# Where the attention block's output stage meets the second MLP: sixteen transposes put ahead of fifteen filling products, and shift and scale given out by whole PSUM tiles

## The chip, the cores and the metric

The kernel runs on one core of a Trainium2 chip. A core has five engines with a queue each: TensorE (PE in the profile), VectorE (DVE), ScalarE (ACT), GpSimd (POOL) and SyncE (SP), the last of which issues nearly all transfers here. Every time is in microseconds (us) of the device; less is better. Before the change three runs took 1163.52, 1165.8 and 1166.83 us; their median is 1165.8 us.

## The reference, cut to what matters

Two layers act on 512 latent tokens and 256 context tokens of width 1024. Layer 0 mixes tokens by pooling, layer 1 by attention; an MLP follows each. The stretch around the change belongs to layer 1 and the latent tokens alone:

```
o_lat = attend(q_l, k_all, v_all).reshape(B, L, D) @ w_o
x     = x + gt1 * rms_norm(o_lat, g_mix_post)
h     = rms_norm(x, g_mlp_pre) * (1.0 + sc2) + sh2      # modulate
m_lat = square(relu(h @ w_mlp_in)) @ w_mlp_out
```

The norm goes over a token's 1024 values, the shift and the scale are per channel. So a row of 128 tokens must have all of its attention output before it can be normalised, and the MLP's first product needs it transposed, with channels on the partitions.

## The kernel before

The 512 latent tokens are four tiles of 128, t = 0 to 3. Float32 operands are split into a coarse part ("hi") and a remainder ("lo"), and each product of 128 channels is three matmuls: hi by hi, hi by lo, lo by hi. ScalarE makes hi by a cast, VectorE makes lo by a subtraction.

`output()` is the output stage. `attn_mm` multiplies the attention result with w_o (line 1403, tile `psy`), `attn_ev` applies the gate and sums squares. Then, tile by tile, `norm_r` adds the residual (VectorE, line 364), `norm_s` sums squares (ScalarE, line 196) and has GpSimd make the reciprocal root (`rs`, line 211), and `norm_c` scales the row into `acc` (ScalarE line 560 or VectorE line 562). For t = 3, the last, `norm_c` is on VectorE.

When two tiles stand ready, `norm_pair` calls `modulated_pair`. It makes 16 transposes of 128x128 (TensorE, line 385) into four PSUM tiles `psx`. Each tile q holds channels 2q and 2q+1 (kk = 0 and 1), each over both token tiles (u = 0 and 1). Eight operations of 128x256 then apply scale and shift and write back to `acc` (VectorE line 393, ScalarE line 396; the tuple `on_act` says which goes where). The two results of tile q overwrite half a row of `acc` (512 columns): q = 0 and 1 the halves of the pair's first token tile, q = 2 and 3 those of its second. So an operation must also wait until the transposes that read those columns are through: q = 1 overwrites what channels 4 to 7 of the first token tile are transposed from. For the last pair (`fine`) each q then gets its own cast to hi (ScalarE, line 399) and subtraction to lo (VectorE, line 400).

The second MLP takes its inner products from `Inner.part` (line 608, tile `psin`), 128x256 each here: chunk 0 is the tokens of pair 0 and 1, chunk 1 those of pair 2 and 3. Since pair (0, 1) is ready earlier, chunk 0 serves as filling while the last pair is normalised: 24 matmuls for each of the two halves of the first weight tile (`first1[0]`) and 24 for the first half of the second (`first1[1]`), 72 in all. All that follows them needs the last pair: 120 more matmuls of 128x256, then `mlp1` with matmuls of 128x512. There, fourteen of the sixteen weight tiles are worked in seven pairs, each with seven products (`product`, lines 987 to 991; tile `pso`), whose sums ScalarE stores for the first pair (line 989) and VectorE adds for the others (line 991).

The order of the work comes from two things. The program is written with a table of times (`at(time, fn)`, run in the order of time), and the framework then schedules the instructions of each engine by its own estimate of their times. Where a list `ordered` holds True, `Kept` marks each TensorE instruction so that it stays in the order of the program; such instructions carry line 87 in the profile. In `output()` it held False. `norm_pair` of the last pair stood at 47.4, and the filling of `first1[1]` behind it at 47.5 and 47.6.

Of the kernel before, what the change touches and what calls it, by code (L numbers as in the profile page):

```python
# [19 lines left out]
KT = D // P  # L20
# [44 lines left out]
class Steps:  # L65
# [3 lines left out]
    def at(self, t, fn, *args):  # L69
        self.items.append((t, len(self.items), fn, args))  # L70
# [20 lines left out]
def backbone(ctx: ExitStack, tc, x, ctx_in, w_ada, w_pool, pool_scale, w_qkv, g_q, g_k, w_o, w_mlp_in,  # L91
             w_mlp_out, vecs, rope, band, out):
    nc = tc.nc
    ordered, mixed = [False], [False]
# [48 lines left out]
    def raw_load(src, pool=None):  # L143
        if pool is None and turns:
            pool = (pools[0], rawp)[turns.pop(0)]
        t = (pool or pools[0]).tile([P, 2048], F32, tag="raw", name="raw")
        d = sy.dma_start(t, src)
        if pinned[0]:
            tc.keep_in_program_order(d)
        return t  # L150
# [12 lines left out]
    def split(raw, hi, lo, pin=False, q=None):  # L163
        if q is not None:
            raw, hi, lo = (z[:, 512 * q:512 * q + 512] for z in (raw, hi, lo))
        a = sc.copy(hi, raw)  # L166
        if pin:
            tc.keep_in_program_order(a)
        b = ve.tensor_tensor(out=lo, in0=raw, in1=hi, op=ALU.subtract)  # L169
        if pin:  # L170
            tc.keep_in_program_order(b)
# [248 lines left out]
    def mod0(t, q, on_act):  # L420
        ci, ps = 0 if t < NL else 1, turned[t, q]
        for kk in range(2):
            k = 2 * q + kk
            sa, b = avec[0][1][:, k, ci:ci + 1], mods[0][:, SH2 * KT + k, ci:ci + 1]
            h, src = accv[:, t:t + 2, k * P:(k + 1) * P], ps[:, kk, :].rearrange("p (u n) -> p u n", n=P)
            if on_act:
                sc.activation(h, src, AF.Identity, scale=sa, bias=b)
            else:
                ve.tensor_scalar(out=h, in0=src, scalar1=sa, scalar2=b, op0=ALU.mult, op1=ALU.add)
        ks = slice(2 * q, 2 * q + 2)  # L430
        h = accv[:, t:t + 2, 2 * q * P:(2 * q + 2) * P].rearrange("p u (k n) -> p k u n", n=P)
        turned[t, q] = (h, *(z.rearrange("p k (h q n) -> p k q h n", h=2, n=P)[:, ks, t // 2] for z in (hH, hL)))
# [329 lines left out]
    def w_in(i, g, rg, pin=False, wait=None):  # L762
        return rg.load(w_mlp_in[i, g], 256, pin, wait)
# [49 lines left out]
    def halved(t, q, part):  # L813
        h, hi, lo = turned[t, q]
        if part:
            ve.tensor_tensor(out=lo, in0=h, in1=hi, op=ALU.subtract)
        else:
            sc.copy(hi, h)

    def keep(store, key, fn, *args):  # L820
# [16 lines left out]
        h=lambda t, act, q: mod0(t, q, act), xhi=lambda t, q: halved(t, q, 0), xlo=lambda t, q: halved(t, q, 1))  # L837
# [391 lines left out]
    def last0(st, n, t):  # L1229
# [18 lines left out]
        if n == 5:  # L1248
            st.at(18.4, rope_load)
            st.at(44, rope_tables)  # L1250
            st.at(5.5, lambda: split(*raw0[0], True))
            raws = []
            st.at(31.3, w_chunk, 2, 1, raws)
            for q in range(4):
                st.at(31.3 + q / 1000, lambda q: split(*raws[0], q=q), q)
            st.at(52, w_chunk, 0, 0, raws)
            st.at(52.01, lambda: split(*raws[1], True))
            st.at(61, w_chunk, 0, 1, raws)
            st.at(61.01, lambda: split(*raws[2], True))
            st.at(61.1, w_chunk, 1, 0, raws)  # L1260
            st.at(61.11, lambda: split(*raws[3], True))
            st.at(83, w_chunk, 1, 1, raws)
            st.at(83.01, lambda: split(*raws[4], True))
            attention(st, 97.4, 2.7)
            output(st, 97.4 + 2.7 * 43.691)
# [150 lines left out]
    first1, raw1 = [], []  # L1416
# [38 lines left out]
    def output(st, base):  # L1455
        at, halves = lambda i, fn, *args: st.at(base + i, fn, *args), []
        for n, (ch, t) in enumerate(((0, 0), (0, 1), (1, 0), (0, 2), (1, 1), (0, 3), (1, 2), (1, 3))):
            b = 5.2 * n
            at(b, attn_mm, ch, t)
            at([5.2, 10.4, 15.6, 20.8, 26, 31.2, 36.4, 41.6][n], attn_ev, ch, t)  # L1460
            if ch:
                at([16.9, 27.3, 37.7, 42.9][t], norm_r, t, (False, False, False, False)[t])
                at([17.9, 28.3, 38.7, 43.9][t], norm_s, t, (False, False, False, False)[t])
                at([18.814, 29.214, 39.614, 46.4][t], norm_c, t, (False, True, True, False)[t])
                if t % 2:
                    at(36.3 if t == 1 else 47.4, norm_pair, t - 1, 1, 1, h1H, h1L, t == 1, t == 3,
                       ((False, True, True, False, True, False, True, False), (True, False, True, False, True, False, True, False))[t // 2], halves if t == 1 else None)

        def upper_half():
            hi, lo, h = halves[0]  # L1470
            tc.keep_in_program_order(sc.copy(hi, h))
            ve.tensor_tensor(out=lo, in0=h, in1=hi, op=ALU.subtract)

        at(41.65, upper_half)
        for f in range(2):
            for h in range(2):
                at(41.7 + f / 10 + h, lambda *a: first1[0].part(*a), 0, f, range(4 * h, 4 * h + 4))
        parts[1] = small.tile([P, 32], F32, tag="part", name="part", bufs=1)
        for j in range(4):
            at((7, 12, 17, 25)[j], ada_sum, 1, GT2, j, 1, parts[1][:, 8 * j:8 * j + 8])  # L1480
        raws = []
        at(20, lambda: first1.append(Inner(0, w_in(1, 0, early, False, raws), h1H, h1L, None, chunks1, LAT, True)))
        at(32, lambda: split(*raws[0]))
        at(26, lambda: raw1.append(raw_load(w_mlp_in[1, 1], rawp).rearrange("p (k n) -> p k n", n=256)))
        at(36, half_early)
        for h in range(2):
            at((47.5, 47.6)[h], lambda ks: first1[1].part(0, 0, ks), range(4 * h, 4 * h + 4))

    def fin_b(t):
        y = yg.pop(t)  # L1490
# [94 lines left out]
```

## Time and profile before

| what | us |
|---|---|
| median of three runs | 1165.8 |
| the profiled execution, as timed | 1165.75 |
| its span, first to last instruction | 1163.9 |
| around the span | 1.85 |
| TensorE busy | 1143.8 (98%) |
| VectorE busy | 933.6 (80%) |
| ScalarE busy | 628.5 (54%) |
| granted TensorE clock, mean | 0.996 |

Busy times are sums over the span. A matmul is listed with its whole passage through the array, while the next one starts before its end; so the distance between two starts is what a matmul costs in a row of them. In a row of the timeline the first number is the start, the second the time from the first start to the last end of the group, and brackets give the engine's idle time ahead of the group with what ended it.

### The profile page before, as it was taken

How to read it: one execution, taken by the hardware profiler on the slowest of the kernel's cores; microseconds unless marked ns; L12 is line 12 of the kernel's file. 1: busy time of each engine (PE TensorE's matmuls, PEld its weight loads, DVE VectorE, ACT ScalarE, POOL GpSimd, SP SyncE). 2: the span in 40 equal slices, each digit the busy share in tenths (PEclk: the TensorE clock that was granted, in tenths of full speed). 3: DMA queues.
4: the chain of work that ended last, by engine and by line, in shares of the span. 5: the costliest groups of instructions: out<-in, count | busy, mean ns of one | idle time of the engine just before them, and what ended most of it. 6: DMA issues, size and time to landing. Idle time of an engine off the chain costs nothing.

```text
span 1163.9 us, 15946 instructions
## 1 busy us (share of the span) xinstructions
PE 1143.8 (98%) x6172; PEld 993.2 (85%) x6172; DVE 933.6 (80%) x1515; ACT 628.5 (54%) x1068; POOL 70.0 (6%) x120
## 2 busy tenths in 40 slices
PE   7999999999999999999999999999999999999997
PEld 5679889998898988998888889988988888888886
DVE  4688688998988997996778699867688779778876
ACT  5687555554354534555675367743676436534522
POOL 2130000000000000000241200002000000000001
PEclk9999999999999999999999999999999999999999
DMA  9964223343334444343522002125234214313312
GB/s 372 419 251 168 73 85 105 142 145 122 132 145 145 145 145 145 109 145 109 181 73 73 37 1 73 37 77 210 76 133 157 75 70 145 109 41 140 109 39 106
DMA packets 25516, 147.32 MB, mean 127 GB/s; under 512 B 2785, under 2 KB 5217, under 8 KB 9698
## 3 DMA queue, kind: packets, MB, share of 16 engines
q1 hardware_dynamic: 25442, 146.32, 34.5%
q8 instruction: 48, 0.79, 0.3%
q14 instruction: 26, 0.21, 0.1%
HBM read 138.96 MB, written 7.34 MB: 126 GB/s over the span
## 4 chain that ended last, share of the span: by engine, by line
PE 62%; issue 30%; DVE 2%; POOL 2%; ACT 2%; DMA 1%; POOLq 0%; SPq 0%; DVEq 0%; ACTq 0%
PE pso L878 22%; PE psin L732 18%; PE psy L1403 3%; PE po L1378 3%; PE pss L1337 3%; PE psq L1133 2%; PE pspt L1359 2%; PE pspool L87 2%; PE psin L87 1%; PE psin L608 1%; PE psada L87 1%; DMA raw<-in_w_ada 1%; PE psm L87 1%; PE psg L87 1%; POOL rs L211 1%
## 5 line engine op out<-in xcount | busy, mean ns | idle before, releaser
L878 PE MATMUL pso<-units,rb 128*128 128x512 f32 x1152 | 278.9, 392 | 0.0
L878 PEld LDWEIGHTS pso<-units,rb 128*128 128x128 f32 x1152 | 214.7, 188 | 41.1
L301 DVE SCALAR_TENSOR_TENSOR rows<-raw,cond,rows 128x256 f32<-128x256 f32 x280 | 127.3, 479 | 2.0
L890 DVE TENSOR_TENSOR acc<-acc,pso 128x512 f32<-128x512 f32 x129 | 85.5, 677 | 41.9 <-PE pso L878 41.6
L608 PE MATMUL psin<-ra,rb 128*128 128x512 f32 (+1 forms) x320 | 91.4, 363 | 1.4 <-ACT ra L399 1.4
L987 PE MATMUL pso<-units,pairs 128*128 128x512 f32 x336 | 82.3, 389 | 0.0
L608 PE MATMUL psin<-ra 128*128 128x512 f32 (+1 forms) x256 | 76.2, 376 | 0.0
L987 PEld LDWEIGHTS pso<-units,pairs 128*128 128x128 f32 x336 | 63.1, 188 | 13.1
L991 DVE TENSOR_TENSOR acc<-acc,pso 128x512 f32<-128x512 f32 x72 | 48.8, 684 | 26.5 <-PE pso L987 26.5
L608 PEld LDWEIGHTS psin<-ra,rb 128*128 128x128 f32 x320 | 58.4, 193 | 10.3 <-ACT ra L399 1.6
L209 POOL TENSOR_SCALAR ms<-ss 128x1 f32<-128x1 f32 x16 | 10.5, 655 | 939.1 <-ACT junk L196 925.4
L732 PE MATMUL psin<-ra,units 128*128 128x384 f32 x336 | 65.5, 337 | 0.4 <-ACT psin L744 0.4
L732 PE MATMUL psin<-sums,units 128*128 128x384 f32 x336 | 64.0, 337 | 0.0
L732 PEld LDWEIGHTS psin<-ra,units 128*128 128x128 f32 x336 | 59.8, 188 | 3.9 <-ACT psin L744 0.5
L169 DVE TENSOR_TENSOR units<-raw,units 128x1024 fp32r<-128x1024 f32 (+2 forms) x49 | 55.1, 1152 | 8.6 <-ACT units L166 8.4
L732 PEld LDWEIGHTS psin<-sums,units 128*128 128x128 f32 x336 | 59.0, 188 | 1.6
L608 PE MATMUL psin<-rb 128*128 128x512 f32 (+1 forms) x160 | 58.0, 363 | 0.2 <-DVE rb L400 0.2
L166 ACT CAST units<-raw 128x1024 fp32r<-128x1024 f32 (+2 forms) x49 | 46.9, 996 | 17.9 <-PE pso L878 13.7
L608 PEld LDWEIGHTS psin<-ra 128*128 128x128 f32 x256 | 47.1, 188 | 8.7
L888 ACT COPY acc<-pso 128x512 f32<-128x512 f32 x48 | 27.1, 586 | 48.2 <-PE pso L878 47.7
L1133 PE MATMUL psq<-units,ra 128*128 128x512 f32 x216 | 52.2, 393 | 0.0
L608 PE MATMUL psin<-rb,ra 128*128 128x512 f32 (+1 forms) x128 | 48.1, 376 | 0.0
(282 smaller groups left out, 2384.8 us busy)
## 6 DMA issues: line engine op xcount, KB each, us to landing
raw<-in_w_ada SPq DMA_DIRECT2D x48, 1024.0 KB, 5.0
raw<-in_w_mlp_in SPq DMA_DIRECT2D x32, 1024.0 KB, 4.8
raw<-in_w_mlp_out SPq DMA_DIRECT2D x32, 1024.0 KB, 5.7
raw<-in_w_qkv SPq DMA_DIRECT2D x6, 1024.0 KB, 4.8
spill<-xr SPq DMA_DIRECT2D x10, 512.0 KB, 4.1
xr<-spill SPq DMA_DIRECT2D x10, 512.0 KB, 6.7
raw<-in_w_o SPq DMA_DIRECT2D x4, 1024.0 KB, 4.9
xr<-in_x SPq DMA_DIRECT2D x4, 512.0 KB, 5.7
```

Of the source, the lines that this page charges most:

```text
L87: return lambda *args, **kw: self.tc.keep_in_program_order(f(*args, **kw))
L166: a = sc.copy(hi, raw)
L169: b = ve.tensor_tensor(out=lo, in0=raw, in1=hi, op=ALU.subtract)
L301: ve.scalar_tensor_tensor(out=r, in0=raw[:, k, :], scalar=cond[:, k, c:c + 1], in1=r, op0=ALU.mult, op1=ALU.add)
L608: te.matmul(ps[:, bank, o:o + ln], w[:, k, fs], rhs, start=start, stop=(k == KT - 1 and n == 2), skip_group_check=len(ks) < KT or self.paired)
L732: te.matmul(bank, w[k], a[k], start=start and k == 0 and m == 0, stop=stop and k == 3 and m == 2, skip_group_check=True)
L878: te.matmul(pss[h][:, 0:cols[h][1]], a[:, f, ts_], w[:, f, cols[h][0]:sum(cols[h])], start=(n == 0 and not seeded[t]), stop=(n == len(seq) ...
L890: ve.tensor_tensor(out=d, in0=d, in1=ps[:, 0:w], op=ALU.add)
L987: te.matmul(ps, a, w, start=(m == 0), stop=(m == len(seq) - 1))
L991: ve.tensor_tensor(out=M[n][:, t], in0=M[n][:, t], in1=ps, op=ALU.add)
L1133: te.matmul(ps, a[:, k, sl], w[:, k % 4, :], start=(k == 0 and n == 0), stop=(k == KT - 1 and n == 2))
L1337: te.matmul(ps[:, c2, 0:384], a[:, sl], b[:, kv, 384 * c2:384 * c2 + 384], start=(n == 0), stop=(n == 2))
```

## The change

Three things change in `output()`. The shift and scale of the last pair is given out by whole PSUM tiles: q = 0 and 2 to ScalarE, q = 1 and 3 to VectorE, four operations each as before. The filling products of `first1[1]` are cut into 9 (channels 0 to 2), now at 47.3 ahead of the pair's transposes, and 15 (channels 3 to 7), at 47.45 behind them. From 47.35 to 47.5 `ordered` holds True, so that the 16 transposes and the 15 products stay in this order among themselves.

```diff
@@ -1464,7 +1464,7 @@
                 if t % 2:
                     at(36.3 if t == 1 else 47.4, norm_pair, t - 1, 1, 1, h1H, h1L, t == 1, t == 3,
-                       ((False, True, True, False, True, False, True, False), (True, False, True, False, True, False, True, False))[t // 2], halves if t == 1 else None)
+                       ((False, True, True, False, True, False, True, False), (True, True, False, False, True, True, False, False))[t // 2], halves if t == 1 else None)
@@ -1484,7 +1484,9 @@
         for h in range(2):
-            at((47.5, 47.6)[h], lambda ks: first1[1].part(0, 0, ks), range(4 * h, 4 * h + 4))
+            at((47.3, 47.45)[h], lambda ks: first1[1].part(0, 0, ks), (range(3), range(3, KT))[h])
+        for z, on in ((47.35, True), (47.5, False)):
+            at(z, ordered.__setitem__, 0, on)
```

No instruction is added or removed; 16 transposes, 72 filling matmuls, 8 shifts, 4 casts and 4 subtractions remain.

The first place is TensorE around the last pair's transposes. `psin_7421` is the accumulator of `first1[0]`, `psin_7514` (after the change `psin_7478`) that of `first1[1]`, the four `psx` are the pair's tiles. Before:

```order
L608 MATMUL psin_7514<-ra_99,rb_100 128x256 x2
L385 MATMUL psx_7478<-ident_87,acc_86 128x128 x3
L385 MATMUL psx_7483<-ident_87,acc_86 128x128 x3
L385 MATMUL psx_7488<-ident_87,acc_86 128x128 x3
L385 MATMUL psx_7493<-ident_87,acc_86 128x128 x3
L608 MATMUL psin_7514<-rb_100 128x256
L608 MATMUL psin_7514<-ra_99,rb_100 128x256
L608 MATMUL psin_7421<-ra_99,rb_100 128x256
L608 MATMUL psin_7514<-ra_99,rb_100 128x256
L608 MATMUL psin_7421<-rb_100 128x256
```

And now:

```order
L608 MATMUL psin_7421<-ra_99,rb_100 128x256
L87 MATMUL psx_7488<-ident_87,acc_86 128x128 x3
L87 MATMUL psx_7493<-ident_87,acc_86 128x128 x4
L87 MATMUL psx_7498<-ident_87,acc_86 128x128 x4
L87 MATMUL psx_7503<-ident_87,acc_86 128x128 x4
L87 MATMUL psin_7478<-ra_99,rb_100 128x256
L87 MATMUL psin_7478<-rb_100 128x256
L87 MATMUL psin_7478<-ra_99,rb_100 128x256 x2
L87 MATMUL psin_7478<-rb_100 128x256
L87 MATMUL psin_7478<-ra_99,rb_100 128x256 x2
```

Before, the first transpose of each tile (it reads token tile 2 alone) stood further up, in two places, then 70 of the 72 filling matmuls came ahead of the other 12 transposes, and 2 behind. Now one transpose stands further up (behind 33 filling matmuls), 57 filling matmuls come ahead of the other 15, and 15 behind. The third row from the end in the first fence, `psin_7421<-ra_99,rb_100`, is the first product that needs the last pair.

The second place is VectorE's queue for the same pair; the rows with a minus are before's, those with a plus now's.

```order
 L1472 TENSOR_TENSOR rb_100<-acc_86,ra_99 128x4x256
 L562 TENSOR_SCALAR acc_86<-xr_4902,rs_7474 128x1024
-L393 TENSOR_SCALAR acc_86<-psx_7478,avec11_96,mods1_92 128x256
-L393 TENSOR_SCALAR acc_86<-psx_7483,avec11_96,mods1_92 128x256
-L393 TENSOR_SCALAR acc_86<-psx_7488,avec11_96,mods1_92 128x256
-L393 TENSOR_SCALAR acc_86<-psx_7493,avec11_96,mods1_92 128x256
+L393 TENSOR_SCALAR acc_86<-psx_7493,avec11_96,mods1_92 128x256 x2
+L393 TENSOR_SCALAR acc_86<-psx_7503,avec11_96,mods1_92 128x256 x2
 L400 TENSOR_TENSOR rb_100<-acc_86,ra_99 128x2x256 x4
```

Nothing moved past anything else; VectorE reads two whole tiles where it read half of each of four. ScalarE's queue changes in the same way.

The third place is ScalarE in the first pair of `mlp1`: `work_7890` and `work_7918` are the relu of a weight tile's two halves, line 978 their square, line 166 the cast of the next weight tile, line 989 the storing of products.

```order
 L619 ACTIVATE work_7890<-psin_7865 128x512
+L619 ACTIVATE work_7918<-psin_7893 128x512
 L978 ACTIVATE hid_7548<-work_7890 128x512
 L166 CAST ra_99<-raw_7773 128x2048
+L978 ACTIVATE hid_7548<-work_7918 128x512
 L954 CAST ra_99<-work_7859 128x1024
 L989 COPY acc_86<-pso_7777 128x512
```

The second half's relu and square now stand ahead of the first stored product, where they stood behind the fourth and the fifth. The framework's estimate moved some more rows on TensorE, VectorE and ScalarE in the first two pairs of `mlp1`; behind these the order is the same as before.

## The prediction

> **What bounds the kernel now.** I read the page's busy times first, then TensorE's waits from 812 us on (the stage of the change and all that follows), then the windows around the longest of them.
>
> ```profile
> PE 1143.8 (98%) x6172; PEld 993.2 (85%) x6172; DVE 933.6 (80%) x1515; ACT 628.5 (54%) x1068; POOL 70.0 (6%) x120
> ...
> PE psin L608 <- ACT ra L399: 1.4, 1, 1.4
> PE psin L608 <- DVE rb L400: 0.2, 1, 0.2
> ...
> core 0: us, PE busy (x) PEld busy (x) DVE busy (x) ACT busy (x) POOL busy (x), PEclk, DMA share, GB/s
> 819.50:828.40 8.90, 8.90 (x76) 8.87 (x75) 3.98 (x6) 3.18 (x6) 1.72 (x5) 1.00 0.15 61
> 828.40:832.84 4.44, 2.82 (x22) 2.41 (x21) 3.27 (x7) 3.87 (x8) 0.00 (x0) 1.00 0.00 0
> 832.84:836.30 3.46, 3.46 (x19) 3.46 (x18) 3.46 (x4) 2.12 (x3) 0.00 (x0) 0.51 0.11 12
> 836.30:848.00 11.70, 11.70 (x99) 11.70 (x99) 8.44 (x9) 7.16 (x9) 0.00 (x0) 1.00 0.35 125
> 848.00:1140.00 292.00, 292.00 (x1297) 241.52 (x1296) 232.32 (x270) 143.77 (x184) 0.00 (x0) 1.00 0.29 103
> ```
>
> TensorE sets the time. Its only two waits in this stretch are at the joint: for the last pair's hi (line 399), then its lo (line 400). From 848 us to 1140 us it is busy for 292.00 of 292.00 us, so what the joint gives back reaches the end unless a new wait arises. A third loss is not in the list of waits: from 832.84 to 836.30 the granted clock (PEclk) is 0.51.
>
> TensorE's timeline at the joint: psin on line 608 is a filling or a dependent product, psx on line 385 a transpose.
>
> ```profile
> 819.51 0.28 PE L608 MATMUL psin<-ra,rb 128*128 128x256 f32 x1
> ...
> 822.42 0.49 PE L385 MATMUL psx<-ident,acc 128*128 128x128 f32 x3
> ...
> 828.45 1.47 PE L385 MATMUL psx<-ident,acc 128*128 128x128 f32 x12
> 829.67 0.36 PE L608 MATMUL psin<-rb 128*128 128x256 f32 x1
> 829.87 0.28 PE L608 MATMUL psin<-ra,rb 128*128 128x256 f32 x1
> 831.55 0.51 PE L608 MATMUL psin<-ra,rb 128*128 128x256 f32 x2 [1.40 <-ACT ra L399]
> 832.28 0.38 PE L608 MATMUL psin<-rb 128*128 128x256 f32 x1 [0.22 <-DVE rb L400]
> 832.50 0.40 PE L608 MATMUL psin<-ra,rb 128*128 128x256 f32 x2
> ...
> 832.86 0.62 PE L608 MATMUL psin<-ra,rb 128*128 128x256 f32 x2
> ...
> 836.38 0.28 PE L608 MATMUL psin<-rb 128*128 128x256 f32 x1
> ...
> 848.01 0.40 PE L608 MATMUL psin<-ra,rb 128*128 128x512 f32 x1
> ```
>
> At full clock a 128x256 product costs 0.12 us: the 97 from 836.38 to 848.01 take 11.63. A transpose costs 0.10 (12 from 828.45 to 829.67). The product behind transposes takes 0.20 (829.67 to 829.87), so each visit to the transposes costs 0.08 more.
>
> What the other engines do in the meantime:
>
> ```profile
> 825.56 0.75 DVE L562 TENSOR_SCALAR acc<-xr,rs 128x1024 f32<-128x1024 f32 x1 [1.11 <-POOL rs L211]
> 829.57 2.00 DVE L393 TENSOR_SCALAR acc<-psx,avec,mods 128x256 f32<-128x256 f32 x4 [3.26 <-ACT acc L396]
> 831.53 2.50 DVE L400 TENSOR_TENSOR rb<-acc,ra 128x512 fp32r<-128x512 f32 x4
> ...
> 828.97 2.02 ACT L396 ACTIVATE acc<-psx,mods,avec 128x256 f32<-128x256 f32 x4 [4.41 <-PE psx L385]
> 830.88 2.18 ACT L399 CAST ra<-acc 128x512 fp32r<-128x512 f32 x4
> ```
>
> Row 3's norm is done at 825.56 + 0.75 = 826.31, and yet the transposes start at 828.45: filling stands ahead of them in TensorE's queue. Two filling products are left to hide a chain of shift, cast and subtraction that takes 832.16 − 828.45 = 3.7 us.
>
> **What the joint loses, in three terms.** For hi: from 829.87 the next start comes after 1.68 instead of 0.12, so 1.56. For lo: three products from 831.55 to 832.50 take 0.95 instead of 0.36, so 0.59. Half clock: 17 products from 832.86 to 836.38 take 3.52 instead of 2.04, so 1.48. Together 3.63.
>
> **The transposes, moved ahead of 15 products.** 57 filling products and one transpose now come first: 819.51 + 57 × 0.12 + 0.10 + 0.08 = 826.5. Row 3 is there at 826.31, so TensorE meets it 0.2 late and does not wait. Fifteen transposes (1.5) and the visit's 0.08 end at 828.1, and 15 filling products (1.8) last to 829.9. TensorE's work is unchanged but for one visit less (two for three): −0.08.
>
> **Shift and scale by whole tiles.** VectorE used to wait for ScalarE: its first operation starts at 829.57, 0.60 after ScalarE's, and the wait row names ScalarE (3.26). [...] The change takes this wait away, but a new one takes its place: VectorE's first tile, q = 1, overwrites columns that the first token tile's channels 4 and 5 are transposed from, so it needs the tenth of the 15 transposes: 826.5 + 9 × 0.10 + 0.27 (one transpose's passage) + 0.03 = 827.7. ScalarE starts 0.52 behind the transposes as before (828.97 − 828.45), at 827.0.
>
> Hi: ScalarE's four shifts take 1.91 (828.97 to 830.88), so the casts start at 828.9 and the first ends at 829.5. TensorE asks for it at 829.9. The first term, 1.56, goes, with 0.4 to spare.
>
> Lo: VectorE's four shifts take 1.96 (829.57 to 831.53), so the first subtraction starts at 829.7 and ends 0.63 later at 830.3; TensorE saw it 0.12 after its end before (832.16 to 832.28), so at 830.4. It comes for it at 829.9 + 0.24 = 830.15. A wait of 0.28 remains. The lower bound is the pitch that VectorE had in an undisturbed pair of such shifts, 0.45 instead of 0.49,
>
> ```profile
> 815.99 0.99 DVE L393 TENSOR_SCALAR acc<-psx,avec,mods 128x256 f32<-128x256 f32 x2
> ```
>
> which leaves 0.14. I take 0.2, between the two. Later subtractions come every 0.63, while TensorE has 12 products, 1.4 us, for each: no further wait.
>
> **The clock.** In the 3.4 us before 832.84 TensorE did a few transposes, then 2 products, 1.40 of nothing, and some products; then the clock was halved for 3.4 us. Earlier, 14 transposes in a row cost no clock:
>
> ```profile
> 813.19 1.69 PE L385 MATMUL psx<-ident,acc 128*128 128x128 f32 x14
> 814.64 5.03 PE L1403 MATMUL psy<-units,ra 128*128 128x256 f32 x40
> ```
>
> 40 products there take 4.87 us to 819.51, 0.12 each. After the change there are 1.5 us of transposes, 1.8 of products, and 0.2 of waiting, which is nearer to 813.19 than to 828.45 (transposes and waits there: 1.22 + 1.40 + 0.22 = 2.84). I count the 1.48 as won; the other end is 1.7, half of 3.4, lost again.
>
> [...]
>
> **What lies behind the joint.** VectorE's chain moves up by 831.53 − 829.7 = 1.8, TensorE by 3.5; the difference eats slack. Two places are tight enough to be named.
>
> ```profile
> 835.29 0.33 SPq L147 DMA_DIRECT2D raw<-in_w_mlp_in  x1
> ...
> 841.13 1.90 ACT L166 CAST rb<-raw 128x2048 fp32r<-128x2048 f32 x1 [1.57 <-PE psin L608]
> ...
> 843.07 2.29 DVE L169 TENSOR_TENSOR rb<-raw,rb 128x2048 fp32r<-128x2048 f32 x1 [2.06 <-ACT rb L166]
> ...
> raw<-in_w_mlp_in SPq DMA_DIRECT2D x1, 1024.0 KB, 4.8
> ...
> 863.82 0.60 ACT L619 ACTIVATE work<-psin 128x512 f32<-128x512 f32 x1 [1.54 <-DVE pairs L954]
> ...
> 865.47 1.91 ACT L166 CAST ra<-raw 128x2048 fp32r<-128x2048 f32 x1 [0.38 <-DMA raw<-in_w_mlp_in]
> 867.28 1.04 ACT L954 CAST ra<-work 128x1024 fp32r<-128x1024 f32 x1
> 868.22 1.06 ACT L989 COPY acc<-pso 128x512 f32<-128x512 f32 x2
> ...
> 870.25 2.88 PE L987 MATMUL pso<-units,pairs 128*128 128x512 f32 x12
> ```
>
> The weights for 848.01 are loaded when VectorE frees a buffer (835.29, then 833.5), land 4.8 later at 838.3, 0.6 later than TensorE would release their cast (841.13 − 3.5 = 837.6). The split then ends at 845.36 − 3.5 + 0.6 = 842.5, wanted at 844.5: 2.0 to spare where there was 2.65. Next, the first stored product was out at 868.75, and the fifth product tile, which takes over its buffer, starts at 870.25. This chain hangs on a load (0.38 of waiting) and moves up by 2.9, and a square of 0.6 now stands ahead: 868.75 − 2.9 + 0.6 = 866.45 against 870.25 − 3.5 = 866.75. A margin of 0.3: I cost it at nothing, with 0 to 0.6 as bounds. No DMA is added, and SP's and POOL's orders are the same.
>
> **The sum.** −1.56 − 0.59 − 1.48 − 0.08 + 0.2 = −3.5. The profiled execution was timed at 1165.75, within 0.05 of the median, so 1165.75 − 3.5 = 1162.2.
>
> **Rivals.**
>
> *The clock still falls.* Transposes plus the remaining wait make one slow window: 1.7 lost, 1163.9. For it: 1.7 us without products is close to the 1.5 of 813.19 that went well, and where the windows lie against the kernel may differ from one execution to the next. Against: 15 products separate the two parts. Chance 0.07.
>
> *A small new wait behind the joint*, at the buffer with a margin of 0.3 or among the rows that moved in the first two pairs: 0.6 to 2, so 1162.8 to 1164.2. Chance 0.09.
>
> *Slower: a weight load misses its turn.* The ScalarE row at 865.47 already waits for its load, and a relu that needs TensorE now stands ahead of it. If that load waits until the buffer of the step behind it comes free, it slides by one landing, one cast and one subtraction: 4.8 + 1.9 + 2.3 = 9.0. Less 2.0 of slack, TensorE stands for 7.0, long enough to halve the clock for another 1.7: 1162.2 + 8.7 = 1170.9. It decides from a delay of 5.5 on (2.0 of slack and the gain). For it: the ring of raw buffers is short. Against: SP's order is the same, and ScalarE was idle for 1.54 just where the relu goes. Chance 0.10.
>
> *The change doesn't do what it says*, the transposes still behind most of the filling: the orders of before and after exclude it.
>
> **How the numbers follow.** A measurement of this kernel can tell about 0.3% from no change, 3.5 us, so the bound is 1162.3, almost on the forecast. The sum's case has 0.74, 1161.3 to 1162.9. Of it I put 0.58 below the bound: of the three runs two lie at or above the profiled execution, so a typical run of before loses at least as much as this one. The other 0.16, the clock's 0.07, the small wait's 0.09 and 0.01 of the slow rival are within 0.3%: 0.33. Slower keeps 0.09. The range for 8 in 10 goes up to 1164.6, over the clock and the small wait, and down to 1160.8, since single runs lay up to 2.3 below their median.
>
> **What would show it.** Right: transposes (line 87) starting at about 826.5; VectorE's shifts at 827.7 with no wait for ScalarE; no wait for line 399 and at most 0.3 for line 400; clock 1.00 throughout; the first 128x512 product at 844.5. Wrong: a clock of 0.5 in any window from 826 to 840, or any new wait of TensorE between 844 and 920.

## The result, and the profile after

| | before | after |
|---|---|---|
| median, us | 1165.1 | 1162.66 |
| lowest to highest of 22 runs, us | 1163.11 to 1166.83 | 1161.48 to 1164.33 |
| ratio of the runs, with its 95% interval | | 0.9983 (0.9977 to 0.9988) |
| span of the profiled execution, us | 1163.9 | 1159.7 |
| joint: first filling product to first 128x512 product, us | 28.50 (819.51 to 848.01) | 25.95 (817.86 to 843.81) |
| from there to the end of the span, us | 315.89 | 315.89 |

The change makes the kernel faster by 0.12% to 0.23%, about 2.0 us (1165.1 × 0.0017). The two profiled spans differ by more, 4.2 us, since 1.65 of it lies ahead of the joint, in a part of the program that is the same in both: before's profiled execution had a slow window of the clock near its start (PEclk 0.92 from 19 to 40 us, in after 1.00). That varies from one execution of before to the next (the table below has six), so below the joint is compared by its own length. The prediction was 1162.2, in a range of 1160.8 to 1164.6.

TensorE's only wait from 812 us on, and its windows with the granted clock (third number from the end):

```profile
PE psin L608 <- DVE rb L1472: 0.6, 1, 0.6
...
819.50:826.40 6.90, 6.29 (x53) 6.09 (x53) 3.17 (x3) 1.96 (x4) 1.54 (x4) 1.00 0.19 76
...
828.20:830.00 1.80, 1.78 (x15) 1.58 (x14) 1.80 (x4) 1.80 (x4) 0.00 (x0) 1.00 0.00 0
830.00:832.00 2.00, 2.00 (x19) 2.00 (x18) 2.00 (x4) 2.00 (x3) 0.00 (x0) 1.00 0.00 0
```

Both waits at lines 399 and 400 have left the list, the clock stays at 1.00, and there is a wait that wasn't there before, for line 1472. TensorE's timeline of the same stretch, with the transposes now on line 87:

```profile
817.86 0.28 PE L608 MATMUL psin<-ra,rb 128*128 128x256 f32 x1
...
821.85 0.27 PE L87 MATMUL psx<-ident,acc 128*128 128x128 f32 x1
821.87 0.36 PE L608 MATMUL psin<-ra,rb 128*128 128x256 f32 x1
822.84 0.39 PE L608 MATMUL psin<-rb 128*128 128x256 f32 x1 [0.61 <-DVE rb L1472]
823.07 0.40 PE L608 MATMUL psin<-ra,rb 128*128 128x256 f32 x2
...
825.71 1.80 PE L87 MATMUL psx<-ident,acc 128*128 128x128 f32 x15
827.26 0.36 PE L87 MATMUL psin<-ra,rb 128*128 128x256 f32 x1
...
829.14 0.40 PE L608 MATMUL psin<-ra,rb 128*128 128x256 f32 x2
829.55 0.39 PE L608 MATMUL psin<-rb 128*128 128x256 f32 x1
829.77 0.40 PE L608 MATMUL psin<-ra,rb 128*128 128x256 f32 x2
...
843.81 0.40 PE L608 MATMUL psin<-ra,rb 128*128 128x512 f32 x1
```

And VectorE and ScalarE beside it:

```profile
821.57 1.22 DVE L1472 TENSOR_TENSOR rb<-acc,ra 128x1024 fp32r<-128x1024 f32 x1
823.89 0.75 DVE L562 TENSOR_SCALAR acc<-xr,rs 128x1024 f32<-128x1024 f32 x1 [1.10 <-POOL rs L211]
827.00 1.90 DVE L393 TENSOR_SCALAR acc<-psx,avec,mods 128x256 f32<-128x256 f32 x4 [2.36 <-PE psx L87]
828.82 2.48 DVE L400 TENSOR_TENSOR rb<-acc,ra 128x512 fp32r<-128x512 f32 x4
...
826.23 1.93 ACT L396 ACTIVATE acc<-psx,mods,avec 128x256 f32<-128x256 f32 x4 [3.34 <-PE psx L87]
828.04 2.18 ACT L399 CAST ra<-acc 128x512 fp32r<-128x512 f32 x4
```

Line 1472 makes the lo of the first pair's channels 4 to 7. The filling product that reads it first comes at 822.84, 0.97 behind the one ahead of it (821.87), which after a transpose should be 0.20. In before the same product stood later in TensorE's queue, behind 38 products and 4 transposes instead of 34 and 1, and met line 1472 just as it ended (823.23 + 1.22 = 824.45). The product behind it took 0.21 to the next start already there (824.52 to 824.73):

```profile
824.52 0.37 PE L608 MATMUL psin<-rb 128*128 128x256 f32 x1
824.73 0.40 PE L608 MATMUL psin<-ra,rb 128*128 128x256 f32 x2
...
823.23 1.22 DVE L1472 TENSOR_TENSOR rb<-acc,ra 128x1024 fp32r<-128x1024 f32 x1
```

### The profile page after: what moved, and what is told of

Same layout as the page of the kernel before. It is cut to its first block, busy times and chain, and to the rows that moved or that the text cites. A ratio compares the mean times of both kernels' runs of the same rounds, so it can differ in the third digit from the quotient of the medians.

```text
span 1159.7 us, 15945 instructions
## 1 busy us (share of the span) xinstructions
PE 1140.7 (98%) x6172; PEld 990.7 (85%) x6172; DVE 932.7 (80%) x1515; ACT 628.8 (54%) x1068; POOL 69.2 (6%) x120
## 4 chain that ended last, share of the span: by engine, by line
PE 62%; issue 30%; DVE 2%; POOL 2%; ACT 2%; DMA 1%; POOLq 0%; SPq 0%; DVEq 0%; ACTq 0%
PE pso L878 22%; PE psin L732 18%; PE psy L1403 3%; PE po L1378 3%; PE pss L1337 3%; PE psq L1133 2%; PE pspt L1359 2%; PE pspool L87 2%; PE psin L87 1%; PE psin L608 1%; PE psada L87 1%; DMA raw<-in_w_ada 1%; PE psm L87 1%; POOL rs L211 1%; PE psg L87 1%
## 5 line engine op out<-in xcount | busy, mean ns | idle before, releaser
L608 PE MATMUL psin<-ra,rb 128*128 128x512 f32 (+1 forms) x310 | 87.8, 360 | 0.0
L608 PEld LDWEIGHTS psin<-ra,rb 128*128 128x128 f32 x310 | 55.6, 189 | 8.7
L166 ACT CAST units<-raw 128x1024 fp32r<-128x1024 f32 (+2 forms) x49 | 46.9, 996 | 17.0 <-PE pso L878 12.9
```

The costliest lines, as they stand in the source:

```text
L608: te.matmul(ps[:, bank, o:o + ln], w[:, k, fs], rhs, start=start, stop=(k == KT - 1 and n == 2), skip_group_check=len(ks) < KT or self.paired)
```

## The experiments

The main theory: the change is worth what TensorE's new order saves, less the new wait at line 1472; the clock's share counts only where the clock falls. The rivals were the whole tiles as half of the gain, a clock that always falls or falls because of the transposes, and, for a faster version, a chain behind the transposes that sets the end whatever TensorE does.

### Each half of the change by itself

```diff
# e1: before, with whole tiles and nothing else
-    (True, False, True, False, True, False, True, False)
+    (True, True, False, False, True, True, False, False)
# e2: after, with the old split
-    (True, True, False, False, True, True, False, False)
+    (True, False, True, False, True, False, True, False)
```

> The kernel before with the shift and scale given out by whole PSUM tiles and nothing else changed; the transposes stay behind 70 filling products. The joint is measured from the start of the first filling product to the start of the first 128x512 product: 28.50 us before (819.51 to 848.01), 25.95 after (817.86 to 843.81). Theory: the order of TensorE is what the change is worth, and the whole tiles are worth little, because VectorE exchanges its wait for ScalarE (its first shift 1.12 us behind the first of the late transposes before) for a wait on a later transpose (1.29 us behind them after). So the joint is 28.2 to 28.5 where the clock falls in it, 26.7 to 27.0 where it doesn't, and the time is within 0.3 us of before. Rival: the serial use of PSUM tiles by two engines is half of the loss; then the joint is 1.2 us or more shorter and the time about 1164.0.

> The changed kernel with the old split of shift and scale (each PSUM tile shared by both engines). Theory: nearly all of the gain is the order of TensorE. VectorE's first shift comes even earlier than with whole tiles (826.83 against 827.00 on the time axis of the changed kernel), but it then follows ScalarE step by step and ends 0.2 to 0.3 us later, so the joint is 26.1 to 26.3 us against 25.95 and the time 1162.9. Rival (whole tiles are half of the gain): a joint of 27.2 or more, 1164.

Whole tiles alone: 1.0001 of before (0.9991 to 1.0011), a joint of 28.41 with the clock fallen in it (0.58 from 834 to 838 us). TensorE's row and VectorE's:

```profile
832.64 0.51 PE L608 MATMUL psin<-ra,rb 128*128 128x256 f32 x2 [1.31 <-ACT ra L399]
...
830.70 1.90 DVE L393 TENSOR_SCALAR acc<-psx,avec,mods 128x256 f32<-128x256 f32 x4 [3.22 <-PE psx L385]
```

VectorE waits for the transposes now and not for ScalarE, and waits as long (3.22, before 3.26). The order alone: 0.9982 (0.9973 to 0.9990), as fast as both together by the times, and a joint of 25.71, shorter by 0.24 than with whole tiles. That is on the other side of what I expected (26.1 to 26.3). The rows of the order alone tell why:

```profile
828.56 0.61 ACT L399 CAST ra<-acc 128x512 fp32r<-128x512 f32 x1
829.07 0.57 ACT L396 ACTIVATE acc<-psx,mods,avec 128x256 f32<-128x256 f32 x1
...
829.21 0.69 DVE L400 TENSOR_TENSOR rb<-acc,ra 128x512 fp32r<-128x512 f32 x1
829.82 0.54 DVE L393 TENSOR_SCALAR acc<-psx,avec,mods 128x256 f32<-128x256 f32 x1
...
829.79 0.40 PE L608 MATMUL psin<-ra,rb 128*128 128x256 f32 x2
830.02 0.32 PE L608 MATMUL psin<-rb 128*128 128x256 f32 x1
```

With the old split the first channels are complete after one shift on either engine, and the framework puts their cast and subtraction ahead of the fourth shift. So the first lo is ready when TensorE comes for it (no wait at line 400). With whole tiles VectorE does all four shifts first. The gain is the order's; in the new order the whole tiles cost a quarter of a microsecond in the joint, too little for the times to show.

### The clock's share

```diff
# e3: before, with 11 products that nothing reads, where TensorE waits for hi
+        def idle_work():
+            z = first1[1]
+            for n in range(11):
+                te.matmul(z.ps[1][:, 0, 0:256], z.f0[0][:, 0, :], h1H[:, 0, 0:256], start=True, stop=True, skip_group_check=True)
+        for z, on in ((47.55, True), (47.7, False)):
+            at(z, ordered.__setitem__, 0, on)
+        at(47.65, idle_work)
```

> The kernel before with 11 more products of 128x256 on TensorE (1.3 us) where it waits for the last pair's hi, into PSUM columns that the first real product there overwrites; nothing reads them. The wait stays, but TensorE is busy in it. It tells the clock's share of the loss apart from the waits'. Theory: the granted clock falls because TensorE stands idle, and in only about half of the executions of before (its 22 runs lie in three groups, 1163.1 to 1163.5, 1164.2 to 1165.3 and 1165.7 to 1166.8). So here the clock stays 1.00 from 828 to 840, the joint is 27.0 us, the time is 0.7 us below before on the mean, and the group above 1165.5 is gone. Rival 1: the clock falls all the same, since it follows the transposes and not the idle time: joint 28.5, time as before. Rival 2: the clock fell in every execution of before: time 1.5 us below it.

The ratio is 0.9993 (0.9984 to 1.0002), the median 0.6 us below that of before beside it (1163.91 against 1164.47). None of the 11 runs is above 1165.45, where 13 of the 35 runs of before beside it are at 1165.68 or more. The joint is 27.02. Its rows, the twelve products being one filling product and the eleven added:

```profile
829.07 1.59 PE L87 MATMUL psin<-ra,rb 128*128 128x256 f32 x12
...
831.48 0.39 PE L608 MATMUL psin<-rb 128*128 128x256 f32 x1 [0.22 <-DVE rb L400]
```

The long wait is filled, the transposes are all still there, and the clock in the joint is 1.00. That profile alone would say little, since before's clock stays up in some executions too (below). The times say more, although the ratio's interval includes 1: were high times as frequent here as in before (13 of 35), none in 11 runs would come about once in 170 times (22/35 to the 11th power). So what goes with the fall here is the idle time (a row of 1.40 in before, filled in e3), and not the 12 transposes, which stand in one row in both (828.45 in before, 827.64 in e3).

Five more profiled executions of before itself tell how often it falls.

> The kernel before once more, for one profile, to see how often the clock falls in its joint. Theory: the clock's windows lie anywhere against the kernel, and the quiet stretch of the joint makes a slow one in about half of the executions: a joint of 28.4 to 28.5 us with a granted clock near 0.5 for 3.4 us, or of 26.9 to 27.1 with a clock of 1.00. Rival: it falls in every execution, as in the two profiles of this order so far (28.50 and 28.40).

> The same kernel again, with the same two outcomes: a joint of 28.4 to 28.5 us with the fallen clock, or of 26.9 to 27.1 without. If it falls in every execution, all looks show the former; if in half of them, three looks alike have a chance of one in four.

> The kernel before once more for a profile. The looks so far all had the clock fallen in the joint (28.49 us twice, 28.50 in the first profile, 28.40 with whole tiles), all were timed at 1165.5 or more, and all had a slow window at the program's start too (0.92 from 19 to 40 us). Theory: an execution from the lower group (1163.0 to 1163.7) has a clock of 1.00 in the joint and a joint of 27.0 us; so a look timed below 1163.8 shows that, and one at 1165.5 or more shows 28.4 to 28.5. Rival: the clock always falls in the joint and the groups come from the program's start and end alone; then a look below 1163.8 still has a joint of 28.4 to 28.5.

> As the look before it: by the theory a time below 1163.8 goes with a joint of 27.0 us at a clock of 1.00, a time above 1165.5 with 28.4 to 28.5; by the rival the joint is 28.4 to 28.5 in either.

> As the two looks before it, in case these show only one of the groups.

| execution of before | time, us | PEclk 19 to 40 us | joint, us | clock in the joint (830 to 834 us, 834 to 838 us) |
|---|---|---|---|---|
| the profile before | 1165.75 | 0.92 | 28.50 | falls (0.85, 0.72) |
| e5 | 1165.83 | 0.92 | 28.49 | falls (0.83, 0.75) |
| e6 | 1165.55 | 0.92 | 28.49 | falls (0.78, 0.79) |
| e9 | 1163.91 | 0.92 | 27.01 | 1.00 |
| e10 | 1163.02 | 1.00 | 27.03 | 1.00 |
| e11 | 1165.92 | 0.92 | 28.47 | falls (0.89, 0.68) |

The window from 826 to 840 us (clock third from the end) and the row of the wait, of e10 first and then of e11:

```profile
826.00:840.00 14.00, 12.38 (x103) 11.97 (x102) 10.32 (x13) 9.12 (x13) 0.00 (x0) 1.00 0.23 76
...
830.29 0.51 PE L608 MATMUL psin<-ra,rb 128*128 128x256 f32 x2 [1.40 <-ACT ra L399]
```

```profile
826.00:840.00 14.00, 12.38 (x90) 11.97 (x89) 9.62 (x14) 7.98 (x12) 0.00 (x0) 0.88 0.20 76
...
831.71 0.51 PE L608 MATMUL psin<-ra,rb 128*128 128x256 f32 x2 [1.40 <-ACT ra L399]
```

The waits are the same to a hundredth, 1.40 and 0.22, and the clock falls in four of six executions and not in the other two; 103 matmuls against 90 in the same 14 us, transposes counted. The rival that it always falls is out. What my expectation had wrong is the grouping: e9 was timed above 1163.8 with a clock of 1.00 in the joint, because its slow window at the start cost it something of its own (its first filling product starts at 819.17, e10's at 818.25).

What differs between the six is where the slow windows of the clock lie against the joint. The one near the start and the one in the joint are 3.41 us long (34.43 to 37.84 and 833.15 to 836.56 in e11, 34.12 to 37.53 and 832.84 to 836.25 in the profile before) and begin 798.72 us apart in both, 234 times 3.413. The last one, at the program's end, begins 327.68 us behind the one in the joint (at 1160.83 and 1160.52), 96 times 3.413. In e10 and e9 the last one begins at 1157.80 and 1158.77, and none lies in the joint; 327.68 ahead of it a border between two windows would lie at 830.12 in e10 and at 831.09 in e9, an estimate from these distances. From the first filling product the slow window begins after 12.9 to 13.5 in the four with the fall, behind both waits, and the estimated border lies at 11.9 in the other two, inside the long wait. The window that ends at the border, of e11 with the slow one behind it, then of e10:

```profile
829.73:833.14 3.41, 1.79 (x14) 1.38 (x12) 3.40 (x7) 3.41 (x8) 0.00 (x0) 1.00 0.00 0
833.15:836.56 3.41, 3.41 (x19) 3.41 (x18) 3.40 (x5) 1.97 (x3) 0.00 (x0) 0.50 0.04 5
```

```profile
826.70:830.12 3.42, 2.19 (x20) 1.98 (x18) 1.81 (x4) 2.41 (x5) 0.00 (x0) 1.00 0.02 5
```

TensorE is idle for 3.41 − 1.79 = 1.62 us in the first and for 3.42 − 2.19 = 1.23 in the last (1.29 in e9's). The last also has all 12 transposes in it, where the first has only the end of them, and yet it is the first that the half clock follows. So in these six executions the half clock followed where one window, counted in this way, held both waits, and 12 transposes beside 1.23 us of idle time brought no fall in e10. What share of idle time it takes is not shown.

### What the change left, and a faster version

```diff
# e7: after, with the eight transposes of the third token tile first (modulated_pair)
-                for u in range(2):
+                for u in range(1 if fine and not wide else 2):
                     te.transpose(ps[:, kk, u * P:(u + 1) * P], works[u][:, k * P:(k + 1) * P], ident)
             pss.append(ps)
+        if fine and not wide:
+            for k in range(KT):
+                te.transpose(pss[k // 2][:, k % 2, P:2 * P], works[1][:, k * P:(k + 1) * P], ident)
# e8: after, with 12 products ahead and 12 behind
-            at((47.3, 47.45)[h], lambda ks: first1[1].part(0, 0, ks), (range(3), range(3, KT))[h])
+            at((47.3, 47.45)[h], lambda ks: first1[1].part(0, 0, ks), (range(4), range(4, KT))[h])
# e4: e7 and e8 together, and
-                at(41.7 + f / 10 + h, lambda *a: first1[0].part(*a), 0, f, range(4 * h, 4 * h + 4))
+                at(47.46 if f and h else 41.7 + f / 10 + h, lambda *a: first1[0].part(*a), 0, f, range(4 * h, 4 * h + 4))
```

> The changed kernel with one of the three moves of the faster version: the eight transposes of the third token tile come first and together, which fills the wait for line 1472 with work; 9 products stay ahead and 15 behind. Theory: a chain leads from the late transposes over cast and subtraction to the first lo, 3.7 us long here, and only 15 products stand beside it; so the wait at line 1472 is gone, the wait at line 400 grows to about 0.7, and the joint is 25.7 to 25.9 us, nearly the changed kernel's 25.95. Rival: each of the two waits is a loss of its own; then the joint is 25.1 to 25.3.

> The changed kernel with the filling cut into 12 products ahead of the transposes and 12 behind, instead of 9 and 15. Theory (the chain behind the transposes sets the end): three products more ahead shorten the wait for line 1472 by 0.36 and start the transposes no later, three fewer behind lengthen the wait for line 400 by 0.36; the joint stays at 25.9 to 26.0. Rival (each wait is a loss of its own, and the last wait had slack): 25.6.

> The changed kernel with three more moves on TensorE: the eight transposes that read the third token tile alone come first and together, 12 instead of 9 products of the second weight tile ahead of them, and 12 products of the first weight tile's second half behind the other eight transposes, beside the 12 that are left there. Theory: the change left two waits, 0.77 us for the lo of the first pair's upper channels (the filling product at 822.84 waits for line 1472) and 0.17 for the last pair's lo, and both go when other work stands in front of them: no wait of TensorE from 812 us on, a joint of 24.9 to 25.1 us against 25.95, time 1161.7, 0.9 below the changed kernel. Rival: the chain of shift, cast and subtraction behind the last transposes sets the end whatever TensorE does; then the wait at line 400 grows by what the other loses, and the joint stays at 25.8 to 26.0.

e7 has a joint of 25.73 and e8 one of 25.95, as the chain has it and not as if each wait counted by itself. Each was timed in a single run, 1161.37 and 1164.31 us; e8's had a slow clock near its start (PEclk 0.84 from 19 to 40 us), so the joints are compared and not the times. TensorE's waits in e7, then in e8 (in e7 and e4 the line numbers behind the edit are three higher, so 403 is the subtraction of line 400):

```profile
829.44 0.39 PE L611 MATMUL psin<-rb 128*128 128x256 f32 x1 [0.22 <-DVE rb L403]
```

```profile
825.69 0.39 PE L608 MATMUL psin<-rb 128*128 128x256 f32 x1 [0.26 <-DVE rb L1472]
...
832.39 0.38 PE L608 MATMUL psin<-rb 128*128 128x256 f32 x1 [0.32 <-DVE rb L400]
```

In e7 the wait for line 1472 is gone and the loss stands behind the transposes, partly at hi (a start at 828.35, the next at 828.71) and partly at lo; the listed wait is smaller than the 0.7 I expected at line 400, the two together are not. In e8 one wait shrinks (from 0.61 to 0.26) and another appears (0.32), at the same length.

e4 puts 24 products beside that chain instead of 15, and its list has no wait of TensorE from 800 us to the end. Its transposes and the first and last product of the joint's second half:

```profile
823.35 0.49 PE L87 MATMUL psx<-ident,acc 128*128 128x128 f32 x3
823.80 0.71 PE L87 MATMUL psx<-ident,acc 128*128 128x128 f32 x5
825.84 1.09 PE L87 MATMUL psx<-ident,acc 128*128 128x128 f32 x8
...
829.64 0.40 PE L611 MATMUL psin<-ra,rb 128*128 128x256 f32 x2
...
844.04 0.40 PE L611 MATMUL psin<-ra,rb 128*128 128x512 f32 x1
```

The joint is 25.03, the median 1161.5 us, and the ratio to before 0.9974 (0.9965 to 0.9983). It beats both kernels in the joint, as the theory had it (24.9 to 25.1). Its interval overlaps that of the change (0.9977 to 0.9988), so by the times it is faster than before; that it is faster than the change is shown by the joint alone. What remains of the joint is TensorE's own work but for 0.2: the eight transposes start 0.31 behind the product at 825.53, just after row 3's norm is done (line 565 here, 825.03 + 0.75 = 825.78).

## Why the prediction was right or wrong

The time lies in the range and 0.5 us from the forecast. That it came so near is partly luck: the sum starts from an execution timed 0.65 above the median of before's 22 runs (1165.75 against 1165.1), which makes up for part of a gain that was too large, 3.5 us for a measured 2.0. The larger share of the chances (0.58) went to a gain of over 0.3%; the 0.17% measured is the case that had 0.33. The mechanism, filling moved behind the transposes so that both waits shrink, was right. The sum goes wrong at two large steps and a small one.

| term, us | predicted | measured in the joint |
|---|---|---|
| wait for hi | −1.56 | −1.56 |
| wait for lo | −0.59 + 0.2 | −0.59 + 0.27 |
| one visit to the transposes less | −0.08 | 0.00 |
| wait for line 1472 | 0 | +0.79 |
| sum without the clock | −2.03 | −1.09 (the joint itself −1.08, 27.03 to 25.95) |
| clock | −1.48 | −1.48 in four of six executions of before, else 0 |

- **"826.5 … and does not wait."** The step that failed. I counted 57 filling products at 0.12 as if none could wait. Those of channels 4 to 7 read the lo of line 1472, which in before had ended 0.07 ahead of its first reader. Taking four products and three transposes out from ahead of that reader brings it forward by 0.80 (from 5.01 behind the first filling product to 4.98 − 0.77 = 4.21), nearly all of it into a wait of 0.77 (0.97 − 0.20). The product behind it takes 0.22 to 0.23, 0.02 more than it took in before. So the transposes start 7.85 behind the first filling product and not 7.0. I looked for new waits behind the joint and not among the filling that was to cover it.
- **"I count the 1.48 as won."** Right for the profiled execution, too much for the median: the fall is there in four of six executions. With that share the sum is −1.08 − 4/6 × 1.48 = −2.07; with the share of high times (13 of 35) it is −1.63. The ratio gives 2.0, its interval 1.4 to 2.7, which holds both, so the share stays open between them. My argument that two of three runs lay at or above the profiled one showed only that this one was no rarity. The rival that the clock still falls after the change didn't come: 1.00 up to 1150 us in its profile, and its one listed wait, 0.61, is half of the 1.23 that e10's window bore at full clock. The prediction's reading of the window ahead of the fall was off: of the 2.84 us of transposes and waits that it counted, about 1.0 us of transposes lay ahead of that window (832.84 − 3.41 = 829.43). It set transposes and waits against the fall in one sum; here 1.62 us of waiting in 3.41 stood ahead of the fall, and 12 transposes beside 1.23 of waiting, in e10, had none behind them.
- **"Each visit to the transposes costs 0.08 more."** A misreading. The 1.22 from the first of 12 transposes to the next product is eleven steps of 0.11 and a last one of 0.03; with the 0.08 that the product behind takes longer, the last transpose costs 0.11 like the others. A single transpose in before costs that too (822.98 to 823.33 is 0.35, where two products take 0.24). So a visit costs nothing of its own, and one visit less gains nothing:

```profile
822.98 0.28 PE L608 MATMUL psin<-ra,rb 128*128 128x256 f32 x1
823.10 0.27 PE L385 MATMUL psx<-ident,acc 128*128 128x128 f32 x1
823.13 0.36 PE L608 MATMUL psin<-ra,rb 128*128 128x256 f32 x1
823.33 0.28 PE L608 MATMUL psin<-rb 128*128 128x256 f32 x1
```

- **Hi.** Right, with the margin a little larger than thought: the four shifts took 1.81 (826.23 to 828.04) instead of 1.91.
- **Lo.** VectorE's first shift came 1.29 behind the transposes (827.00 − 825.71), predicted 1.2; its four shifts took 1.82, near the shorter pitch that I had as a bound; what is left is 0.17 at the product itself (829.14 to 829.55, 0.41 for 0.24) and 0.10 at the one behind it (829.55 to 829.77). I had not counted that the product behind this wait would cost 0.22 too.
- **Whole tiles.** I priced both halves of the change in one term for lo. Apart, whole tiles gain 0.09 in the old order (28.50 to 28.41) and lose 0.24 in the new one. The wait for ScalarE was real, but what took its place was as long, as the prediction said; that the old split lets the first channels' cast and subtraction go ahead of the last shift I did not see.
- **Behind the joint.** Right: 315.89 us from the first 128x512 product to the end in both profiles, no wait in the rows that moved. The weight load that I had landing 0.6 late for its cast is there, and hidden:

```profile
837.50 1.91 ACT L166 CAST rb<-raw 128x2048 fp32r<-128x2048 f32 x1 [0.76 <-DMA raw<-in_w_mlp_in]
...
839.44 2.29 DVE L169 TENSOR_TENSOR rb<-raw,rb 128x2048 fp32r<-128x2048 f32 x1 [1.26 <-ACT rb L166]
```

  The cast waits 0.76 for its load; the split ends at 841.73, 2.1 ahead of its use at 843.81 (predicted 2.0). The slower rival, a load that misses its turn, and the small new wait behind the joint didn't come.

## What to carry to other kernels

When work is moved forward as a filling, ask of each piece what it reads and when that is ready: a product that used to arrive just after its operand can wait once work ahead of it is taken away (here from 0.07 behind its operand to 0.77 of waiting). A wait can also be only the visible end of a chain; shortening the wait alone (e7, e8) moved the loss and kept the length, and it was won only when more work stood beside the whole chain (e4, which holds the moves of e7 and e8 too; the added work alone was not run). And a loss that hangs on the clock should be counted with the share of executions that show it, which one profile can't tell.

## What the runs showed that I had not expected

A product behind a wait of TensorE takes 0.22 to 0.23 us to the next start instead of 0.12, at each such place here (832.28 to 832.50 before, 822.84 to 823.07 and 829.55 to 829.77 after). A wait also starts late in the list, since its idle time counts from the listed end of the product ahead (0.28 behind that one's start at 829.87, 0.36 at 821.87) and not from where the next one could have started (0.12 and 0.20). So the wait for line 1472 costs 0.77 + 0.10 = 0.87 where its row says 0.61, and before's wait for hi 1.56 + 0.10 = 1.66 where its row says 1.40: in both, 0.26 more.

And with waits equal to a hundredth of a microsecond (1.40 and 0.22) the clock fell to 0.50 in four executions of six, those in which one window of 3.413 us, counted as above, held both of them.
